# An FFN's weight splits: every second low half by ScalarE and an adding transfer, with the residual parked in HBM and two more weight buffers

## The chip, the cores and the metric

The kernel runs on one core of one Trainium2 chip. The metric is device microseconds of one execution. TensorE (PE) multiplies, VectorE (DVE) and ScalarE (ACT) do elementwise work, GpSimd (POOL) and SyncE (SP) issue transfers here, and 16 DMA engines move the data.

## The reference: what is computed

One layer of an encoder over 256 tokens of width 2048, all in float32. A mixing part (attention in a neighbourhood, and a recurrent block), then a SwiGLU feed-forward network (FFN) of width 5632, then an embedding of the layer's own. Each part ends in a normalisation and an addition to the residual `h`:

```
u  = rms_norm(h) @ w_in;  attn, rec = ...;  mixed = concat(norm(attn), norm(rec)) @ w_out
h  = h + rms_norm(mixed, g_mix_post)
fn = rms_norm(h, g_ffn_pre)
ff = (silu(fn @ w_ffn_gate) * (fn @ w_ffn_up)) @ w_ffn_down
h  = h + rms_norm(ff, g_ffn_post)
gate = sigmoid(rms_norm(h, g_ple_pre) @ w_ple_gate)
h  = h + rms_norm(gate * (p @ w_ple_proj), g_ple_post)
```

## The kernel before

**Three products for one.** PE multiplies float32 values in a reduced form, `fp32r`. To keep accuracy each operand is split into a high half (rounded to `fp32r`) and a low half (what is left), and each product is made of three: high by high, low by high, high by low (lines 601 to 603). The activations are split once. The weights are too large for that and are split as they stream through.

**A weight tile's way.** A tile is 512 KB: 128 partitions by two blocks of 512 columns. SP loads it into a raw buffer (`load_stream`, lines 489 and 506). ACT copies it into a high half `wh` (`hi_stream`, line 556). DVE subtracts to get the low half `wl` (`lo_stream`, line 569), which frees the raw buffer. PE uses a full tile in 12 matmuls of 128x512 (`products`) and then frees `wh` and `wl` (`free_w`). There are four raw buffers, three more in the FFN (`MORE_RAWS`, in the space of a gain vector and a spare tile), and four pairs of `wh` and `wl` (`W_BUFS`).

**The FFN.** Its 11 column groups of 512 are done in three parts of 4, 4 and 3. In each part every group has a gate chunk and an up chunk, whose product `mid` is transposed: DVE transposes blocks of 32x32 and 16 transfers of 32 KB move the blocks (`moved`, line 305; POOL issues 16 or 8 of them, SP the others). Then the down products of the part follow. Nine of the groups do a part of their products by a scheme with seven products in place of eight (`four_products`, `two_products`, `one_product`). Its tiles have 6 matmuls instead of 12, and some of its weight tiles are sums that DVE makes of loaded tiles (`sum_stream`, lines 526 to 537).

**What sets the order.** The order in which each engine gets its instructions is written by a planner (`Plan`): every stream is a generator that yields what it will use next (an engine and a cost, a buffer, or an event to wait for). The planner picks the step that can start first by its own clocks, with a bonus or a malus (`late`) for each stream. On the chip each engine then works through its own list in order and waits on semaphores.

**Around the FFN.** After the mix part `next_norm` adds the result to `h`, transposes it and makes the FFN's input halves. `h` (2 MB, a tile of the pool `rs`) is not touched again until the `next_norm` after the FFN.

Of the kernel before, what the change touches and what calls it, by code (L numbers as in the profile page):

```python
# [10 lines left out]
F32 = mybir.dt.float32  # L11
# [5 lines left out]
P = 128  # L17
S = 256
NT = S // P
# [29 lines left out]
W_BUFS = 4  # L49
R_BUFS = 4  # L50
MORE_RAWS = 3
SM_BUFS = 4
LATE = 0.8
EARLY = 3
# [1 line left out]
AHEAD = 5  # L56
ISSUE, LANDING = 160, 1.7
WARM = 9


class Event:
# [154 lines left out]
def layer(ctx: ExitStack, tc: tile.TileContext, a: dict, out: bass.AP):  # L216
# [5 lines left out]
    plan = Plan(wr=R_BUFS, w=W_BUFS, sm=SM_BUFS, acc=4, ev=1, mid=2, bt=2, m2=1, mt=1, sq=1, T=1, T4=1, **{f"wr{k}": 1 for k in range(MORE_RAWS)})  # L222

    def f32(t):
        return t.bitcast(F32)
# [13 lines left out]

    def raw_kind(i):  # L240
        return f"wr{more_raws[i]}" if i in more_raws else "wr"


    g_first = const.tile([P, KD], F32, name="g_first")
# [44 lines left out]
    def moved(e, here, take, tile_of, turn=True, pool=()):  # L289


        if turn:
            flat = e.rearrange("p t n -> p (t n)")
            yield dve(2 * N)
            nc.vector.transpose(out=flat, in_=flat)
        src = e.rearrange("p t (k j b) -> p t k j b", j=4, b=32)
        mT = None
        for j in range(4):
            for i in range(4):
                first = None if mT else take  # L300
                yield ("pool", 1.3, None, first, None) if i in pool else dma(150, take=first)
                if mT is None:
                    mT = tile_of()
                dst = mT.rearrange("p t k (i b) -> p t k i b", b=32)
                (nc.gpsimd if i in pool else nc.sync).dma_start(  # L305
                    dst[32 * j : 32 * j + 32, :, :, i, :],
                    src[32 * i : 32 * i + 32, :, :, j, :],
                )
        done(here)
        return mT.rearrange("p t k q -> p k t q")  # L310
# [230 lines left out]
    def hi_stream():  # L541
        for i in range(len(tiles)):
            at_hi[0] = i
            for j in pieces(i):
                n = j.stop - j.start
                yield ev_raw[i, j.stop]
                if i in big_w:
                    yield big_w[i][2]
                yield act(n * N, take=None if j.start or i in big_w else "w")
                if i in big_w:  # L550
                    his[i], los[i] = big_w[i][0](), big_w[i][1]()
                elif not j.start:
                    his[i] = wp.tile([P, 2, N], F32R, tag="wh", name="wh")
                    los[i] = wp.tile([P, 2, N], F32R, tag="wl", name="wl")
                src = raws[i][:, j, :]
                nc.scalar.copy(his[i][:, 0 : src.shape[1], :] if n == 2 else his[i][:, j, :], src)  # L556
                done(ev_hi[i, j.stop])

    def lo_stream():
        last_sum = max(f[0] for f in fours.values())  # L560
        for i in range(len(tiles)):
            at_lo[0] = i
            for j in pieces(i):
                n = j.stop - j.start
                yield ev_hi[i, j.stop]
                src = raws[i][:, j, :]
                m = slice(j.start, j.start + src.shape[1])
                yield dve(src.shape[1] * N, give=gives.get(i) or raw_kind(i) if j.stop == 2 else None)
                nc.vector.tensor_tensor(  # L569
                    out=los[i][:, m, :], in0=src, in1=f32(his[i][:, m, :]), op=ALU.subtract  # L570
                )
# [828 lines left out]
    def next_norm(sub, nxt, rstd, ev_rstd, g_next):  # L1400
# [49 lines left out]
        nc.vector.tensor_reduce(out=tot, in_=ssh, op=ALU.add, axis=AX.X)  # L1450
        yield from rstd_of(tot, D, rstd, rt)
        done(ev_rstd)

    TURNED = 3

    def turn_h(c, hi, lo, nxt, gname):
# [8 lines left out]
        for b in range(4):  # L1465
            kk = 4 * c + b
            yield from gained_split(
                *(x[:, kk, :].rearrange("p (t q) -> p t q", t=NT) for x in (hi, lo)), mT[:, b],
                col(gname, kk), give="mt" if b == 3 else None,
            )  # L1470
            done(nxt.ev[kk])

    def next_gain(g, ready):
        yield from load_gain(g[1])
# [476 lines left out]
```

## Time and profile before

| what | us |
|---|---|
| median of 3 runs (1174.24 to 1177.76) | 1175.87 |
| span of the profiled execution | 1171.8 |
| PE busy | 1158.1 |
| DVE busy | 819.2 |
| ACT busy | 672.7 |
| POOL busy | 89.1 |

The runs' times lie about 4 us above the span of the profiled execution, which is counted from its first to its last instruction; the page gives no other time of that execution. Over the whole span the DMA engines move 250.90 MB, 214 GB/s on average.

A row of the table of stretches gives, for a stretch in microseconds from the start of the span, the busy time and number of instructions of each engine, the granted clock of PE, the mean share in which the 16 DMA engines were busy (it is a sum of packet times, and can pass 1), and the GB/s moved. A group row gives line, engine, operation, operands, number, then busy time and mean ns, then the idle time ahead and what ended it. A row of the waits gives engine and line, what they waited for, the sum in us, the number of times and the longest. A row of the chain gives start, length, and what it was.

### The profile page before, as it was taken

How to read it: one execution, taken by the hardware profiler on the slowest of the kernel's cores; microseconds unless marked ns; L12 is line 12 of the kernel's file. 1: busy time of each engine (PE TensorE's matmuls, PEld its weight loads, DVE VectorE, ACT ScalarE, POOL GpSimd, SP SyncE). 2: the span in 40 equal slices, each digit the busy share in tenths (PEclk: the TensorE clock that was granted, in tenths of full speed). 3: DMA queues.
4: the chain of work that ended last, by engine and by line, in shares of the span. 5: the costliest groups of instructions: out<-in, count | busy, mean ns of one | idle time of the engine just before them, and what ended most of it. 6: DMA issues, size and time to landing. Idle time of an engine off the chain costs nothing.

```text
span 1171.8 us, 14922 instructions
## 1 busy us (share of the span) xinstructions
PE 1158.1 (99%) x5276; PEld 960.0 (82%) x5276; DVE 819.2 (70%) x997; ACT 672.7 (57%) x891; POOL 89.1 (8%) x163
## 2 busy tenths in 40 slices
PE   9999999999999999999999999999999999999997
PEld 7888888888888878888888887888888888887786
DVE  6678787898468767855567777765677785568565
ACT  6777777875556645554445554544344554456564
POOL 0000000000000203111000203210000302100000
PEclk9999999999999999999999999999999999999999
DMA  8868566446765778687566777778556877754762
GB/s 304 307 176 233 175 191 199 162 162 208 242 241 163 248 240 253 216 243 203 176 233 209 236 250 204 245 213 223 196 200 225 240 223 228 215 190 158 235 222 76
DMA packets 108714, 250.90 MB, mean 214 GB/s; under 512 B 38880, under 2 KB 45792, under 8 KB 108000
## 3 DMA queue, kind: packets, MB, share of 16 engines
q1 hardware_dynamic: 103344, 244.62, 66.3%
q0 software_dynamic: 4864, 4.99, 1.7%
q8 instruction: 41, 0.67, 0.2%
q14 instruction: 33, 0.27, 0.1%
q10 hardware_dynamic: 432, 0.35, 0.1%
HBM read 239.42 MB, written 2.10 MB: 206 GB/s over the span
## 4 chain that ended last, share of the span: by engine, by line
PE 91%; DMA 3%; DVE 3%; ACT 2%; issue 1%; SPq 1%; ACTq 0%; DVEq 0%
PE acc L603 27%; PE acc L602 27%; PE acc L601 27%; PE acc L614 2%; PE acc L612 2%; PE acc L613 2%; DVE wl L569 1%; DMA wr<-in_w_ffn_up 1%; PE tr L286 1%; ACT wh L556 1%; DMA sq<-ev 1%; DMA more<-in_w_ffn_up 1%; DMA xs<-in_xT 0%; PE pg L317 0%; PE pg L318 0%
## 5 line engine op out<-in xcount | busy, mean ns | idle before, releaser
L569 DVE TENSOR_TENSOR wl<-wr,wh 128x1024 fp32r<-128x1024 f32 (+1 forms) x320 | 383.2, 1210 | 172.1 <-ACT wh L556 168.6
L556 ACT CAST wh<-wr 128x1024 fp32r<-128x1024 f32 (+1 forms) x320 | 332.4, 1044 | 256.9 <-PE acc L602 203.9
L603 PE MATMUL acc<-wl,hT_mix_hi 128*128 128x512 f32 x560 | 218.3, 390 | 2.9 <-DVE wl L569 2.9
L602 PE MATMUL acc<-wh,hT_mix_lo 128*128 128x512 f32 x560 | 218.1, 389 | 0.3 <-DVE hT_mix_lo L275 0.3
L601 PE MATMUL acc<-wh,hT_mix_hi 128*128 128x512 f32 x560 | 218.2, 390 | 0.0
L305 POOL DMA_DIRECT2D mT<-mid x152 | 87.9, 585 | 916.8 <-DMA wr<-in_w_ffn_gate 529.0
L603 PEld LDWEIGHTS acc<-wl,hT_mix_hi 128*128 128x128 f32 x560 | 105.1, 188 | 26.3 <-DVE wl L569 4.5
L603 PE MATMUL acc<-wl,hT_hi 128*128 128x512 f32 x320 | 124.8, 391 | 0.1
L601 PE MATMUL acc<-wh,hT_hi 128*128 128x512 f32 x316 | 124.4, 394 | 0.0
L602 PEld LDWEIGHTS acc<-wh,hT_mix_lo 128*128 128x128 f32 x560 | 105.1, 188 | 22.7 <-DVE hT_mix_lo L275 1.0
L602 PE MATMUL acc<-wh,hT_lo 128*128 128x512 f32 x316 | 123.2, 390 | 0.0
L601 PEld LDWEIGHTS acc<-wh,hT_mix_hi 128*128 128x128 f32 x560 | 105.1, 188 | 21.5
L556 ACT CAST wh<-more 128x1024 fp32r<-128x1024 f32 x60 | 63.3, 1054 | 69.5 <-PE acc L602 64.6
L569 DVE TENSOR_TENSOR wl<-more,wh 128x1024 fp32r<-128x1024 f32 x60 | 72.8, 1221 | 38.9 <-ACT wh L556 36.6
L603 PEld LDWEIGHTS acc<-wl,hT_hi 128*128 128x128 f32 x320 | 60.1, 188 | 13.5 <-DVE wl L569 0.8
L602 PEld LDWEIGHTS acc<-wh,hT_lo 128*128 128x128 f32 x316 | 59.4, 188 | 11.7
L601 PEld LDWEIGHTS acc<-wh,hT_hi 128*128 128x128 f32 x316 | 59.4, 188 | 11.4
L556 ACT CAST wh<-ple 128x1024 fp32r<-128x1024 f32 x27 | 28.5, 1055 | 39.5 <-PE acc L602 34.0
L569 DVE TENSOR_TENSOR wl<-third,wh 128x1024 fp32r<-128x1024 f32 x31 | 37.9, 1221 | 17.8 <-ACT wh L556 17.1
L556 ACT CAST wh<-third 128x1024 fp32r<-128x1024 f32 x31 | 32.7, 1053 | 30.0 <-PE acc L602 23.9
L601 PE MATMUL acc<-wh,mid0h 128*128 128x512 f32 x128 | 49.8, 389 | 0.0
L602 PE MATMUL acc<-wh,mid0l 128*128 128x512 f32 x128 | 49.8, 389 | 0.0
(338 smaller groups left out, 1963.2 us busy)
## 6 DMA issues: line engine op xcount, KB each, us to landing
wr<-in_w_in SPq DMA_DIRECT2D x77, 512.0 KB, 4.6
wr<-in_w_ffn_gate SPq DMA_DIRECT2D x58, 512.0 KB, 4.6
wr<-in_w_ffn_up SPq DMA_DIRECT2D x58, 512.0 KB, 4.6
wr<-in_w_ffn_down SPq DMA_DIRECT2D x57, 512.0 KB, 4.2
wr<-in_w_out SPq DMA_DIRECT2D x32, 512.0 KB, 4.3
wr<-in_w_ple_gate SPq DMA_DIRECT2D x32, 512.0 KB, 4.6
more<-in_w_ffn_down SPq DMA_DIRECT2D x21, 512.0 KB, 4.2
more<-in_w_ffn_gate SPq DMA_DIRECT2D x20, 512.0 KB, 4.7
```

The costliest lines, as they stand in the source:

```text
L286: nc.tensor.transpose(tr[:, b, t * P : (t + 1) * P], e[:, t, sl], ident)
L305: (nc.gpsimd if i in pool else nc.sync).dma_start(dst[32 * j : 32 * j + 32, :, :, i, :], src[32 * i : 32 * i + 32, :, :, j, :],)
L556: nc.scalar.copy(his[i][:, 0 : src.shape[1], :] if n == 2 else his[i][:, j, :], src)
L569: nc.vector.tensor_tensor(out=los[i][:, m, :], in0=src, in1=f32(his[i][:, m, :]), op=ALU.subtract)
L601: nc.tensor.matmul(accs[t], hi[:, sl], his[i][:, j, :], start=st, stop=False, **group)
L602: nc.tensor.matmul(accs[t], lo[:, sl], his[i][:, j, :], start=False, stop=False, **group)
L603: nc.tensor.matmul(accs[t], hi[:, sl], los[i][:, j, :], start=False, stop=sp, **group)
L612: nc.tensor.matmul(dst, x[0], wh, start=start, stop=False, skip_group_check=seeded)
L613: nc.tensor.matmul(dst, x[1], wh, start=False, stop=False, skip_group_check=seeded)
L614: nc.tensor.matmul(dst, x[0], wl, start=False, stop=stop, skip_group_check=seeded)
```

## The change

For every second full weight tile of the FFN (from the fifth tile after the start of the seven-product scheme, `by_dma`), DVE no longer makes the low half. ACT, after its copy to the high half, writes the negated high half into `los[i]` (an activation with scale -1, which gives the raw buffer back), and POOL then issues a DMA that reads the same weight tile from HBM again and adds it into `los[i]`. That gives weight minus high half. There are 101 such tiles.

Two more pairs of weight buffers are used from the same tile on until 24 tiles ahead of the end of the FFN's list (`more_w`, `LAST_W`). They lie in the space of `h`, four halves of 4 KB per partition: `h` is written to HBM after the mix part (`spill_h`) and read back into a new tile when PE has used the last tile of the added buffers (`reload_h`). The `next_norm` after the FFN waits for that.

The planner's cost of a move on POOL goes from 1.3 to 0.65 us, and an accumulation is planned with 1.0 us on POOL and a landing 2.5 us later than the planner's usual latency. PE's instructions and their order stay.

```diff
+MORE_W = 2
+ACCUMULATED = 2
+LAST_W = 24
...
+ACC_ISSUE, ACC_LANDING = 1.0, 2.5
+MOVE_ISSUE = 0.65
...
+    def w_kind(i):
+        return f"w{more_w[i]}" if i in more_w else "w"
+
+    def w_tiles(i):
+        if i not in more_w:
+            return [wp.tile([P, 2, N], F32R, tag=t, name=t) for t in ("wh", "wl")]
+        if "w" not in t2:
+            t2["w"] = t2["pool"].tile([P, 4 * MORE_W, N], F32R, tag="h", name="w")
+        k = 4 * more_w[i]
+        return t2["w"][:, k : k + 2, :], t2["w"][:, k + 2 : k + 4, :]
...
-                yield ("pool", 1.3, None, first, None) if i in pool else dma(150, take=first)
+                yield ("pool", MOVE_ISSUE, None, first, None) if i in pool else dma(150, take=first)
...
+                if i in more_w:
+                    yield ev_spilled
+                yield act(n * N, take=None if j.start or i in big_w else w_kind(i))
...
                 nc.scalar.copy(his[i][:, 0 : src.shape[1], :] if n == 2 else his[i][:, j, :], src)
+                if i in by_dma:
+                    yield act(n * N, give=raw_kind(i))
+                    nc.scalar.activation(los[i], src, AF.Copy, scale=-1.0)
+                    plan.add(accumulated(i), plan.now, -2 * SOON)
                 done(ev_hi[i, j.stop])
+
+    def accumulated(i):
+        yield ("pool", ACC_ISSUE, None, None, None)
+        nc.gpsimd.dma_start(los[i], by_dma[i], accum_op=ALU.add)
+        plan.now += ACC_LANDING
+        done(ev_lo[i, 2])
...
                 yield ev_hi[i, j.stop]
+                if i in by_dma:
+                    continue
...
     def free_w(i):
         if i not in keep:
-            plan.free["w"].append(plan.clk["pe"])
+            plan.free[w_kind(i)].append(plan.clk["pe"])
+        if more_w and i == max(more_w):
+            plan.add(reload_h(), plan.clk["pe"], -SOON)
...
-        yield ev_h
+        yield ev_h if sub is mix else ev_back
...
+        if sub is mix:
+            for e in nxt.ev:
+                yield e
+            plan.add(spill_h(), plan.now)
...
+    def spill_h():
+        yield dma(2048)
+        nc.sync.dma_start(spill, t2["h"])
+        done(ev_spilled)
+
+    def reload_h():
+        yield dma(2048)
+        t2["h"] = t2["pool"].tile([P, NT, D], F32, tag="h", name="h")
+        nc.sync.dma_start(t2["h"], spill)
+        done(ev_back)
...
+    for i in range(min(fours) + 4, i_ple - LAST_W):
+        n += 1
+        if n % (W_BUFS + MORE_W) < MORE_W:
+            more_w[i] = n % (W_BUFS + MORE_W)
+    n = 0
+    for i in range(min(fours) + 4, i_ple):
+        tl = tiles[i]
+        if isinstance(tl, tuple) and i not in fours and i - 1 not in fours:
+            n += 1
+            if n % ACCUMULATED == 0:
+                w, k, n0 = tl
+                by_dma[i] = a[w][n0 // N, k // 2]
```

More of the change, by code (lines that the diff above doesn't have):

```diff
@@ L221, in layer @@
     ps = ctx.enter_context(tc.tile_pool(name="ps", bufs=4, space=bass.MemoryType.PSUM))
-    plan = Plan(wr=R_BUFS, w=W_BUFS, sm=SM_BUFS, acc=4, ev=1, mid=2, bt=2, m2=1, mt=1, sq=1, T=1, T4=1, **{f"wr{k}": 1 for k in range(MORE_RAWS)})
+    plan = Plan(wr=R_BUFS, w=W_BUFS, sm=SM_BUFS, acc=4, ev=1, mid=2, bt=2, m2=1, mt=1, sq=1, T=1, T4=1, **{f"{w}{k}": 1 for w, n in (("wr", MORE_RAWS), ("w", MORE_W)) for k in range(n)})
     def f32(t):
@@ L241, in raw_kind @@
         return f"wr{more_raws[i]}" if i in more_raws else "wr"
+    more_w = {}
+    by_dma = {}
+    def w_kind(i):
[7 more added lines that the diff above has]
+        return t2["w"][:, k : k + 2, :], t2["w"][:, k + 2 : k + 4, :]
     g_first = const.tile([P, KD], F32, name="g_first")
@@ L548, in hi_stream @@
                     yield big_w[i][2]
-                yield act(n * N, take=None if j.start or i in big_w else "w")
+                if i in more_w:
+                    yield ev_spilled
+                yield act(n * N, take=None if j.start or i in big_w else w_kind(i))
                 if i in big_w:
@@ L552, in hi_stream @@
                 elif not j.start:
-                    his[i] = wp.tile([P, 2, N], F32R, tag="wh", name="wh")
-                    los[i] = wp.tile([P, 2, N], F32R, tag="wl", name="wl")
+                    his[i], los[i] = w_tiles(i)
                 src = raws[i][:, j, :]
                 nc.scalar.copy(his[i][:, 0 : src.shape[1], :] if n == 2 else his[i][:, j, :], src)
+                if i in by_dma:
+                    yield act(n * N, give=raw_kind(i))
+                    nc.scalar.activation(los[i], src, AF.Copy, scale=-1.0)
+                    plan.add(accumulated(i), plan.now, -2 * SOON)
                 done(ev_hi[i, j.stop])
+    def accumulated(i):
[3 more added lines that the diff above has]
+        done(ev_lo[i, 2])
     def lo_stream():
@@ L1471, in turn_h @@
             done(nxt.ev[kk])
+    spill = ctx.enter_context(
+        tc.tile_pool(name="spill", bufs=1, space=bass.MemoryType.DRAM)
+    ).tile([P, NT, D], F32, name="h_spill")
+    ev_spilled, ev_back = Event(), Event()
+    def spill_h():
[7 more added lines that the diff above has]
+        done(ev_back)
     def next_gain(g, ready):
@@ L1837, in layer @@
                 more_raws[i] = n % (R_BUFS + MORE_RAWS)
+    n = 0
[3 more added lines that the diff above has]
+            more_w[i] = n % (W_BUFS + MORE_W)
+    n = 0
+    for i in range(min(fours) + 4, i_ple):
[5 more added lines that the diff above has]
+                by_dma[i] = a[w][n0 // N, k // 2]
     for i, (last, _, _, _) in fours.items():
```

## The prediction

> **What bounds the kernel now.** I read the page's totals first, then busy time by stretch, then who waits for whom.
>
> ```profile
> span 1171.8 us, 14922 instructions
> ...
> PE 1158.1 (99%) x5276; PEld 960.0 (82%) x5276; DVE 819.2 (70%) x997; ACT 672.7 (57%) x891; POOL 89.1 (8%) x163
> ...
> PE 91%; DMA 3%; DVE 3%; ACT 2%; issue 1%; SPq 1%; ACTq 0%; DVEq 0%
> ```
>
> PE is busy for all but 13.7 us, and 91% of the chain that ended last is PE. A busy PE could still be a slow one, so the next view gives matmuls by stretch: the FFN from 384 to 1066 us, cut at its up/gate and down phases (528 to 620, 785 to 877 and 998 to 1066 are the three down phases), and three stretches of the input projection with heavy loading.
>
> ```profile
> core 0: us, PE busy (x) PEld busy (x) DVE busy (x) ACT busy (x) POOL busy (x), PEclk, DMA share, GB/s
> 28.00:38.00 10.00, 10.00 (x46) 8.27 (x45) 5.40 (x7) 8.28 (x13) 0.00 (x0) 1.00 1.02 415
> 26.00:46.00 20.00, 20.00 (x90) 16.57 (x89) 12.07 (x14) 15.48 (x23) 0.00 (x0) 1.00 0.93 350
> 0.00:50.00 50.00, 48.77 (x215) 40.27 (x216) 29.41 (x40) 36.29 (x53) 1.20 (x11) 1.00 0.89 317
> ...
> 384.00:1064.00 680.00, 677.10 (x2984) 559.69 (x2983) 465.44 (x475) 340.10 (x370) 87.92 (x152) 1.00 0.72 221
> 384.00:528.00 144.00, 142.13 (x625) 116.90 (x624) 101.64 (x108) 74.84 (x82) 27.88 (x48) 1.00 0.76 238
> 528.00:620.00 92.00, 92.00 (x407) 76.20 (x406) 54.18 (x54) 42.90 (x47) 4.61 (x8) 1.00 0.67 206
> 620.00:785.00 165.00, 163.97 (x723) 135.49 (x723) 121.75 (x124) 87.53 (x95) 27.72 (x48) 1.00 0.76 229
> 785.00:877.00 92.00, 92.00 (x407) 76.20 (x407) 57.04 (x59) 39.62 (x40) 4.61 (x8) 1.00 0.67 206
> 877.00:998.00 121.00, 121.00 (x536) 100.22 (x535) 89.27 (x91) 63.32 (x67) 18.50 (x32) 1.00 0.73 226
> 998.00:1066.00 68.00, 68.00 (x302) 56.32 (x301) 42.86 (x46) 33.82 (x46) 4.61 (x8) 1.00 0.64 197
> ```
>
> In a down phase 407 matmuls take 92.00 us, 0.226 us each, at a granted clock of 1.00 and without a gap; the other FFN rows give the same pace. So the FFN has 680.00 - 677.10 = 2.9 us of idle PE, and that is the most that any help to ACT, DVE or the loads can win there. DVE, which the change relieves, is busy 465 of 680 us and ACT 340: neither is the bound. Who waits, in the FFN:
>
> ```profile
> PE acc L603 <- DVE wl L569: 2.9, 3, 1.4
> ```
> ```profile
> SPq L489 <- DVE wl L569: 455.9, 215, 7.4
> ```
> ```profile
> 716.82 1.06 ACT wh L556
> ...
> 717.90 1.24 DVE wl L569
> ...
> 719.89 0.70 DVE wr L537
> ...
> 720.61 6.03 DMA wr<-in_w_ffn_up
> ...
> 728.10 1.23 DVE wl L569
> ...
> 729.37 0.50 PE acc L603
> ```
>
> The 2.9 us are three stalls. The chain ahead of the one at 729 shows their make: a raw buffer comes free late (719.89 plus 0.70), its load then takes 6.03 us, and the low half reaches PE late. SP's row says that loads always wait for DVE to free a raw buffer.
>
> **The change, part by part.** PE's instructions stay the same and in the same order: 0 us.
>
> *The low halves.* Of the FFN's full tiles, every second one loses its L569 subtraction: 101 tiles (56 of up, 44 of down, 1 of the embedding). Each gets a second ACT copy with scale -1 and an accumulating DMA from POOL that reads the tile's 512 KB from HBM again.
>
> ```profile
> L569 DVE TENSOR_TENSOR wl<-wr,wh 128x1024 fp32r<-128x1024 f32 x314 | 379.2, 1220 | 171.3 <-ACT wh L556 167.8 <-PE acc L603 1.3
> L556 ACT CAST wh<-wr 128x1024 fp32r<-128x1024 f32 x314 | 328.7, 1052 | 255.7 <-PE acc L602 203.9 <-DMA wr<-in_w_ple_gate 8.9 <-PE acc L613 7.5
> L305 POOL DMA_DIRECT2D mT<-mid x152 | 87.9, 585 | 916.8 <-DMA wr<-in_w_ffn_gate 529.0 <-DVE mid L295 235.5 <-DMA more<-in_w_ffn_gate 129.4
> ```
>
> DVE: 101 x 1.22 = 123 us less, of 465. ACT: 101 x 1.05 = 106 us more, 446 of 680. POOL: 101 issues at the 0.585 us of a move, 59 us more, 147 of 680. All three stay under the 680 us of PE work, which covers them; uncovered, ACT's 106 us would be the price, and that needs ACT to be full. The raw buffer of such a tile is freed by ACT's copy instead of by DVE.
>
> *What the DMA engines get.* The trace has no accumulating DMA. From below it costs what a load costs: 512 KB of transfer, 101 x 0.524 = 53 MB. From above I count two loads, because the add must read the weights and what lies in the tile: 106 MB of engine time. I take the upper one, since one transfer and one read of the same size is nearest to two load rows. In MB per us this adds to the rows above, by the phase in which the tiles fall (15, 15, 25, 16, 18, 12 tiles), with 1.049 MB a tile:
>
> - 384 to 528: 238 + 109 = 347, and 362 with the parked residual (2.1 MB)
> - 528 to 620: 206 + 171 = 377
> - 620 to 785: 229 + 159 = 388
> - 785 to 877: 206 + 182 = 388
> - 877 to 998: 226 + 156 = 382
> - 998 to 1066: 197 + 185 + 31 (the residual's 2.1 MB back) = 413
>
> What can the engines do? The row from 26 to 46 moves 350 GB/s at a share of 0.93, which makes 350/0.93 = 376 at a full share; the 50 us row makes 317/0.89 = 356; the best 10 us reach 415. I take 376, the middle one. (The FFN's own 221/0.72 = 307 is no limit, since the rows above exceed it; its shares hold latencies too.) Where demand exceeds 376 over a whole phase, no buffer helps, and PE gets its tiles at the rate of the transfers. The phases grow by 92 x 0.3% = 0.2, 165 x 3.2% = 5.3, 92 x 3.2% = 2.9, 121 x 1.6% = 1.9 and 68 x 9.8% = 6.7 us: 17.0 us. By 356 the six terms are 2.4, 5.4, 14.8, 8.3, 8.8, 10.9 = 51 us; by 415, or with one load's cost instead of two (at most 229 + 79 = 308, or 320 with the residual), 0.
>
> [...]
>
> *The longer way to a low half.* PE now waits for a transfer instead of a DVE subtraction.
>
> ```profile
> wr<-in_w_ffn_down SPq DMA_DIRECT2D x57, 512.0 KB, 4.2
> mT<-mid POOLq DMA_DIRECT2D x152, 32.0 KB, 6.2
> ```
> ```profile
> L489 SPq DMA_DIRECT2D wr<-in_w_ffn_down x57: 327/328/689, 509.7 to 1044.4; - x57
> ...
> DMA to landing us min/median/max: 3.3/4.5/9.3
> ```
> ```profile
> POOL mT L305 <- DMA mT<-mid: 19.7, 20, 2.1
> ```
>
> From PE's release of a weight buffer: high half 1.05, negated copy 1.05, some 0.3 of hand-overs, then from issue to landing 4.5 us (a load's median) at least, 9.3 (its longest) at most; I take the median plus a second reading of 0.524 MB at 376 GB/s, 1.4 us: 5.9. That makes 8.3 us (6.9 to 11.7). What PE gives: with six buffers the five tiles between take 12 matmuls of 0.226 each (6 where two tiles share a seven-product step), 9.9 us at seven places and 11.3 to 14.0 elsewhere, counted to the third matmul, which first reads the low half. In the last 24 tiles there are four buffers again: 3 x 2.71 + 0.45 = 8.6 us. So 8.3 fits everywhere, with 0.3 us to spare in the tail: 0 us. At 11.7 the tail loses 3.1 us in each turn of its four buffers, 6 x 3.1 = 19, and the seven places 7 x 1.8 = 13: 32 us. POOL's queue is in order: an accumulation behind 11 moves (6.4 us, and waits of up to 2.1 us for earlier moves to land) would miss 11.3 us; the order written puts it ahead of them, after five at most (2.9 us).
>
> *Residual and buffers.* The write after the mix stage and the read near the end are counted in the first and last phase. SP's weight loads queue behind each; 2.1 MB is 5.6 us at 376. Raw tiles run some eight tiles (21.7 us) ahead, which covers it; uncovered, 5.6 us each. The read is needed only after the last down tile, some 60 us later. High halves that use the new buffers wait for the write on ACT; the planner puts them 30 tiles into the FFN, after it: 0.
>
> *The stalls.* Earlier free raw buffers help where the transfers have room, which is the first phase: 144.00 - 142.13 = 1.9 us won. The stall at 729 lies in a phase that I count as full and stays.
>
> **Sum.** 1171.8 + 17.0 - 1.9 = 1186.9 us of span. The median of the runs, 1175.87, is 4.1 us above the profiled span; with that, 1191.
>
> **The rivals.**
>
> *Hidden (no change).* The accumulation costs a load, or the engines hold 400 and more. For it: 415 GB/s over 10 us, and PE without a gap at shares of 0.76. Against it: 350 is the best over 20 us. Everything lands in time, and 1.9 to 2.9 us of stalls go: 1173 to 1174 (up to 1179 with a stray stall). [...]
>
> *Late, not full (slower).* The transfers have room, but an accumulation lands later than 8.6 us allows in the tail and 9.9 at the seven places: 1175.9 + 10 to 32 = 1186 to 1208. For it: 6.2 us for 32 KB on POOL's queue, 0.3 us to spare. Against it: the load median. It decides from 6.2 us of issue to landing.
>
> *Faster by over 0.3% (3.5 us).* All 2.9 us of FFN stalls go, and with DVE less loaded also some 0.7 us of those after 1066 us: 1172. Against it: it needs all of them.
>
> **How the numbers follow.** About 0.3% is what a measurement of this kernel can tell. Full engines 0.42 (own range 1180 to 1227, and 1191 within it), late 0.20, hidden 0.32, faster 0.06. Slower is 0.42 + 0.20 = 0.62. The range goes from the hidden case with all stalls gone, 1172, to 356 GB/s with part of the late case, 1175.9 + 51 + 5 = 1232.
>
> **What would show it.** A DMA share of 0.9 or more in the down phases; idle PE of 5 to 10% there, put down to the accumulating DMA or to loads of wr; landing of in_w_ffn_down on POOL's queue near 6 us; no stall at 432 and 472. Right would be more PE idle in the last phase than in the first. Wrong: shares under 0.85 with PE gapless (hidden), or stalls in the last 24 tiles only at shares under 0.85 (late). An accumulation that takes three transfers' time would put the time beyond 1232.

## The result and the profile after

The changed kernel takes 1249.03 us (median of 4 runs, 1247.5 to 1252.56) against 1176.3 us before on the same chip: a ratio of 1.0626, 95% interval 1.0601 to 1.0651. It is 73 us slower. The forecast was 1191 us, and its range ended at 1232.

First the page's totals of the changed kernel: span, busy time by engine, the two queues that carry data (packets, MB, share of 16 engines over the span; q1 is SP's, q0 is POOL's), and the chain that ended last.

```profile
span 1246.2 us, 15098 instructions
...
PE 1182.5 (95%) x5276; PEld 969.7 (78%) x5276; DVE 698.9 (56%) x896; ACT 762.9 (61%) x992; POOL 180.9 (15%) x264
...
q1 hardware_dynamic: 103632, 248.81, 59.8%
q0 software_dynamic: 19408, 57.95, 24.0%
...
PE 60%; DMA 22%; issue 12%; DVE 2%; ACT 2%; POOL 2%; SPq 0%; POOLq 0%; DVEq 0%; ACTq 0%
```

DVE lost 120 us of work, where the prediction counted 123. ACT gained 90 (106) and POOL 92 (59), since an accumulation's issue takes 0.87 us and not the 0.585 of a move. DMA now holds 22% of the chain, which was 91% PE. The same two queue rows of the kernel before:

```profile
q1 hardware_dynamic: 103344, 244.62, 66.3%
q0 software_dynamic: 4864, 4.99, 1.7%
```

q0 gained 52.96 MB, 101 transfers of 512 KB. Its packets' time rose from 0.017 x 16 x 1171.8 = 319 to 0.240 x 16 x 1246.2 = 4785 us summed over the engines, so an accumulation costs 44.2 us of engine time. A load costs 0.663 x 16 x 1171.8 / 244.62 x 0.524 = 26.6 us, by the mean of all that its queue moves. By single packets of 4 KB, the median is 0.328 us for an adding one and 0.159 us for a loading one.

Next, busy time by stretch in the FFN, with the new limits of its phases. The down products start at 543.8, 821.8 and 1052.4 us, so 544 to 645, 822 to 923 and 1052 to 1143 are the down phases:

```profile
core 0: us, PE busy (x) PEld busy (x) DVE busy (x) ACT busy (x) POOL busy (x), PEclk, DMA share, GB/s
384.00:544.00 160.00, 148.87 (x622) 120.39 (x621) 83.92 (x92) 90.16 (x99) 42.79 (x64) 0.96 0.97 282
544.00:645.00 101.00, 95.76 (x412) 78.50 (x411) 36.07 (x38) 57.08 (x63) 17.94 (x23) 0.97 0.97 266
645.00:822.00 177.00, 168.52 (x720) 136.42 (x719) 91.74 (x99) 108.79 (x119) 50.56 (x73) 0.98 1.02 287
822.00:923.00 101.00, 95.48 (x411) 78.23 (x411) 39.14 (x44) 54.59 (x57) 18.91 (x24) 0.97 0.94 267
923.00:1052.00 129.00, 121.89 (x532) 98.99 (x531) 64.94 (x71) 75.61 (x82) 34.06 (x49) 1.00 1.01 285
1052.00:1143.00 91.00, 76.41 (x324) 60.20 (x323) 32.85 (x43) 47.44 (x63) 15.40 (x20) 0.98 0.92 250
384.00:1143.00 759.00, 706.93 (x3012) 572.73 (x3011) 348.66 (x383) 433.68 (x479) 179.67 (x253) 0.98 0.98 276
```

The share of the DMA engines went from 0.72 to 0.98. PE idles in every phase, 52 us in all, most in the last one (14.6 of 91 us), and the granted clock is below 1.00 in five of the six. Who waits, and how long transfers take from issue to landing (median, last column):

```profile
PE acc L635 <- DMA wl<-in_w_ffn_down: 23.1, 10, 5.2
PE acc L635 <- DMA w<-in_w_ffn_up: 17.5, 10, 3.5
PE acc L635 <- DMA wl<-in_w_ffn_up: 5.8, 7, 2.3
PE acc L635 <- DVE wl L601: 3.7, 4, 2.8
```
```profile
wr<-in_w_ffn_gate SPq DMA_DIRECT2D x58, 512.0 KB, 7.2
wr<-in_w_ffn_up SPq DMA_DIRECT2D x58, 512.0 KB, 6.7
wr<-in_w_ffn_down SPq DMA_DIRECT2D x57, 512.0 KB, 7.7
...
wl<-in_w_ffn_up POOLq DMA_DIRECT2D x32, 512.0 KB, 9.2
wl<-in_w_ffn_down POOLq DMA_DIRECT2D x32, 512.0 KB, 8.3
```

An accumulation lands 8.4 us after its issue (median; 7.3 to 13.9), and the loads of `wr` beside it went from between 4.2 and 4.6 us to between 6.7 and 7.7 us. The first packet of an accumulation starts 3.7 us after the issue (median), and its packets spread over another 4.

Last, what the lost time is made of. I took all of the FFN's matmuls, from the first product of its input to the first product behind it, and compared each gap between two starts with the 0.227 us of a matmul at full pace. Before, gaps of 0.23 us too much or more (stalls) make 3.8 us; after, 59.6 us in 38 stalls, 53.7 of them at tiles whose low half an accumulation makes. Another 14.0 us are 70 matmuls 0.427 us apart. The chain shows the first and the last of eleven such matmuls behind the longest stall (start, length, what):

```profile
571.30 8.27 DMA wl<-in_w_ffn_down
...
579.62 0.80 PE acc L635
580.41 0.43 PE acc L633
...
585.10 0.23 PE acc L635
```

So the FFN's 74 us (718.9 to 793.0) are 56 us more of stalls, nearly all on accumulated low halves, 14 us of half pace behind them, and some 4 us of smaller gaps. Of the 53.7 us, 16 lie at the tiles of the tail, which have four buffers, 15 at six tiles whose transfer POOL issued 1.8 to 4.1 us late, 10 at two tiles for which ACT's queue was held, and 12 at thirteen others. Measured by their own matmuls (the first from the FFN's first product on, the last to the first product behind the FFN), the six phases grew by 17, 8, 13, 8, 9 and 19 us.

The half pace goes with a granted clock of 0.50. Two stretches, the first with the stall that ends at 451.6 us, show it (columns as above):

```profile
448.42:451.83 3.41, 1.30 (x6) 0.81 (x5) 3.41 (x4) 3.41 (x5) 0.00 (x0) 1.00 1.05 300
451.83:455.24 3.41, 3.41 (x9) 2.66 (x9) 0.41 (x2) 0.25 (x1) 0.87 (x1) 0.50 1.03 317
```

### The profile page after: what moved, and what is told of

Same layout as the page of the kernel before. It is cut to its first block, busy times and chain, and to the rows that moved or that the text cites. A ratio compares the mean times of both kernels' runs of the same rounds, so it can differ in the third digit from the quotient of the medians.

```text
span 1246.2 us, 15098 instructions
## 1 busy us (share of the span) xinstructions
PE 1182.5 (95%) x5276; PEld 969.7 (78%) x5276; DVE 698.9 (56%) x896; ACT 762.9 (61%) x992; POOL 180.9 (15%) x264
## 4 chain that ended last, share of the span: by engine, by line
PE 60%; DMA 22%; issue 12%; DVE 2%; ACT 2%; POOL 2%; SPq 0%; POOLq 0%; DVEq 0%; ACTq 0%
PE acc L635 18%; PE acc L634 17%; PE acc L633 17%; DMA wl<-in_w_ffn_down 6%; DMA wl<-in_w_ffn_up 6%; DMA w<-in_w_ffn_up 4%; DMA mT<-mid 2%; DVE wl L601 1%; PE acc L645 1%; PE acc L644 1%; PE acc L646 1%; POOL mT L324 1%; DMA third<-in_w_ffn_up 1%; PE tr L305 1%; DMA w<-in_w_ffn_down 1%
## 5 line engine op out<-in xcount | busy, mean ns | idle before, releaser
L576 ACT CAST wh<-wr 128x1024 fp32r<-128x1024 f32 (+1 forms) x279 | 288.2, 1041 | 202.9 <-PE acc L634 127.9
L601 DVE TENSOR_TENSOR wl<-wr,wh 128x1024 fp32r<-128x1024 f32 (+1 forms) x234 | 279.6, 1207 | 182.9 <-ACT wh L576 174.7
L635 PE MATMUL acc<-wl,hT_mix_hi 128*128 128x512 f32 x376 | 148.7, 395 | 9.5 <-DMA wl<-in_w_ffn_up 5.8
L634 PE MATMUL acc<-wh,hT_mix_lo 128*128 128x512 f32 x376 | 147.4, 392 | 0.3 <-DVE hT_mix_lo L294 0.3
L633 PE MATMUL acc<-wh,hT_mix_hi 128*128 128x512 f32 x376 | 147.4, 392 | 0.0
L635 PE MATMUL acc<-w,hT_mix_hi 128*128 128x512 f32 x184 | 75.9, 413 | 17.6 <-DMA w<-in_w_ffn_up 17.5
L633 PE MATMUL acc<-w,hT_mix_hi 128*128 128x512 f32 x184 | 74.5, 405 | 0.0
L634 PE MATMUL acc<-w,hT_mix_lo 128*128 128x512 f32 x184 | 74.2, 403 | 0.0
L576 ACT CAST w<-wr 128x1024 fp32r<-128x1024 f32 x41 | 43.0, 1049 | 38.9 <-PE acc L634 28.2
L635 PEld LDWEIGHTS acc<-w,hT_mix_hi 128*128 128x128 f32 x184 | 36.3, 197 | 29.7 <-DMA w<-in_w_ffn_up 22.2
L601 DVE TENSOR_TENSOR wl<-more,wh 128x1024 fp32r<-128x1024 f32 x27 | 32.9, 1222 | 43.6 <-ACT wh L576 43.4
```

Of the source, the lines that this page charges most:

```text
L601: nc.vector.tensor_tensor(out=los[i][:, m, :], in0=src, in1=f32(his[i][:, m, :]), op=ALU.subtract)
L633: nc.tensor.matmul(accs[t], hi[:, sl], his[i][:, j, :], start=st, stop=False, **group)
L634: nc.tensor.matmul(accs[t], lo[:, sl], his[i][:, j, :], start=False, stop=False, **group)
L635: nc.tensor.matmul(accs[t], hi[:, sl], los[i][:, j, :], start=False, stop=sp, **group)
```

## The experiments

Two theories at first. **A, full engines:** the adding doubles the engines' time, loads come late as a whole, and PE gets tiles at the transfers' rate. **B, lateness:** each accumulation lands after PE wants it, at its own place, and the way it takes through the in-order queues of POOL and ACT decides. All ratios are to the kernel before on the same chip, with 95% intervals.

### The adding taken away, the residual alone, half the transfers, no tail

```diff
-        nc.gpsimd.dma_start(los[i], by_dma[i], accum_op=ALU.add)
+        nc.gpsimd.dma_start(los[i], by_dma[i])
```

> The changed kernel with the adding transfer turned into a plain one of the same 512 KB on the same queue (the low half then holds the weights themselves, so the result is not the layer's; the work of all engines is otherwise the same). Theory A, the second read fills the DMA engines: a packet of 4 KB falls from 0.33 to 0.16 us, the share of the DMA engines in the FFN falls from 0.98 to under 0.88, and the time to 1173 to 1185 us. Theory B, not the engines but the way through POOL is long (issue, first packet some 3.5 us later, landing): an accumulation lands after 7.4 us instead of 8.7, the tail with four buffers keeps at least 8 of its 17 us of stalls, and the time is 1195 to 1225 us.

1189.53 us, 1.0114 (1.0086 to 1.0143). Of 73 us, 60 go with the adding alone; the queue, the order of instructions and the bytes written are the same. Its q0 row and landings:

```profile
q0 software_dynamic: 19408, 57.95, 15.0%
...
wr<-in_w_ffn_up SPq DMA_DIRECT2D x58, 512.0 KB, 5.1
...
wl<-in_w_ffn_up POOLq DMA_DIRECT2D x32, 512.0 KB, 7.0
```

A copying transfer takes (0.150 x 16 x 1187.8 - 319) / 101 = 25.1 us of engine time against 44.2. Stalls fall to 18.6 us. The time lies above what A gave and below what B gave, and of neither theory did the sign come as it was put: the FFN's share is 0.91, not under 0.88, and a landing is 7.0 us, below the 7.4 of B. The adding sets both the engines' time and the landing, so this run can't part the two.

```diff
-            if n % ACCUMULATED == 0:
+            if n % ACCUMULATED == ACCUMULATED:
```

> Only the parked residual, the two more weight pairs and the planner's new cost of a move; no accumulation, DVE makes all low halves. Both theories: the accumulations carry the loss, so 1173 to 1177 us, with one or two of the three stalls of before gone. If parking or the added buffers carry a part of the loss, over 1180 us.

1175.37 us, 0.9988 (0.9973 to 1.0002): the parked residual and the two added pairs cost nothing and bring nothing.

```diff
-ACCUMULATED = 2
+ACCUMULATED = 4
```

> Every fourth full tile accumulates instead of every second (50 instead of 101). Theory A: transfers with the second read counted fall to some 310 MB per us and stay under what the engines reached in the changed kernel (346), so nearly all stalls go but those of the tail: 1178 to 1195 us. Theory B: half of the late tiles stay late, so half of the loss: 1205 to 1218 us.

1216.93 us, 1.0349 (1.0313 to 1.0384). With 50 accumulations 40 of the 73 us are still there, as B had it; a capacity that is merely exceeded at 101 would have set most of it free. A landing still takes 8.2 us.

```diff
-    for i in range(min(fours) + 4, i_ple):
+    for i in range(min(fours) + 4, i_ple - LAST_W):
         tl = tiles[i]
```

> Every second full tile accumulates, but none of the last 24, which have four buffers. Both theories: the 17 us of stalls in the last down phase go and a part of the half-speed matmuls there, 1228 to 1236 us. If the four buffers are the main cause of the loss, under 1210; if the tail's stalls only make up for waits that come later anyway, over 1242.

1228.93 us, 1.0436 (1.0389 to 1.0484), as expected: the 12 accumulations of the tail, where there are four buffers, cost 20 us.

### One place of lateness at a time

In the changed kernel ACT makes the high half, then the negated copy. Here the two are exchanged, so that the transfer is issued about 1 us earlier:

```diff
-                nc.scalar.copy(his[i][...], src)
                 if i in by_dma:
-                    yield act(n * N, give=raw_kind(i))
                     nc.scalar.activation(los[i], src, AF.Copy, scale=-1.0)
                     plan.add(accumulated(i), plan.now, -2 * SOON)
+                    yield act(n * N, give=raw_kind(i))
+                nc.scalar.copy(his[i][...], src)
```

> The changed kernel with the negated copy ahead of the copy to the high half, so that each adding transfer is issued some 1.0 us earlier; bytes, engines and order otherwise the same. Theory A, the DMA engines are full over whole phases: nothing is won, 1244 to 1253 us. Theory B, each transfer is late against the fixed lead that the weight buffers give (8.6 to 14 us from release to use, 10.1 to 13.4 needed where PE stalls): each of the 29 stalls at an accumulated tile shrinks by up to 1.0 us, 24 us in all, and some half-speed matmuls behind them go: 1212 to 1230 us.

1237.63 us, 1.0518 (1.0464 to 1.0573): 11 us less, where B gave 19 to 37 and A nearly nothing. The FFN's stalls fall from 59.6 to 53.0 us.

```diff
-LAST_W = 24
+LAST_W = 8
```

> The two added weight pairs stay in use until 8 tiles ahead of the end instead of 24, so the last down phase has six buffers too, and the residual is read back later. Theory B: the lead there grows from 8.6 to 14 us and most of the 17 us of stalls go: 1228 to 1238 us. Theory A: the last phase has as many bytes as before, its stalls stay: 1244 to 1255 us.

1243.9 us, 1.058 (1.0548 to 1.0612): only 5 us, next to A's range. The stalls of the first tail tiles went, and others came: one of 2.0 us where ACT's queue was held for 10.2 us, and two of 3.0 and 3.6 us near the end.

Where ACT's queue is held, a view of its instructions in the changed kernel shows best (start, length, instruction, and in brackets the idle time before it):

```profile
555.70 1.05 ACT L579 ACTIVATE wl<-wr 128x1024 fp32r<-128x1024 f32 x1
567.00 1.14 ACT L286 CAST mid0h<-mT 128x512 fp32r<-128x512 f32 x2 [10.25 <-DMA wr<-in_w_ffn_down]
568.05 2.00 ACT L576 CAST wh<-wr 128x1024 fp32r<-128x1024 f32 x2
569.95 1.05 ACT L579 ACTIVATE wl<-wr 128x1024 fp32r<-128x1024 f32 x1
```

ACT stands 10.25 us at a copy of `mT`, which the moves fill (the load named is the one that landed last by the profile; the copy reads `mT` alone). Three weight copies queue behind it, and the negated copy that ends at 571 leads to the 5.40 us stall at 579.6. In the next kernel such copies get a due time 10 us later:

```diff
-            plan.add(carried(mid, kk0, mT), plan.now + (0.5 if soon else 3.0), -SOON if soon else SOON)
+            plan.add(carried(mid, kk0, mT), plan.now + (10.0 if soon else 3.0), -SOON if soon else SOON)
```

> The planner takes the copies of the last transposed mid block of a part for ready 10 us after the moves instead of 0.5, so they stand later in ACT's list. Theory B with ACT's queue blocked (8 to 9 us from release to high half at the stalls of 5.4 and 4.9 us early in the first two down phases): these two stalls and the half-speed matmuls behind them go, 1230 to 1240 us. If the block is only a sign of full engines, the stalls move elsewhere: 1244 to 1253 us.

1233.75 us, 1.0483 (1.0457 to 1.0509): 15 us, as B had it. The stalls of 5.40 and 4.88 us are gone.

```diff
-            mT = yield from moved(e, there, "mt", mT_tile, pool=(0, 2) if soon else range(4))
+            mT = yield from moved(e, there, "mt", mT_tile, pool=())
```

> All moves of mid blocks are issued by SP, none by POOL, so no accumulation waits behind a move or for its landing. Theory B: the six accumulations that POOL issued 1.8 to 4.1 us late come in time, 12 to 16 us of stalls go: 1232 to 1240 us, less if the weight loads behind the moves on SP come late; then 1245 to 1260 us.

1265.7 us, 1.0769 (1.0744 to 1.0795): 17 us worse, and above both ranges. With the moves in SP's queue, among its loads, ACT stands 81 us at its copies of `mT`, against 44 in the changed kernel, so the high halves behind them are held longer. To relieve POOL's queue at the cost of SP's did not pay.

### Places mended together

> The changed kernel with two of its places of lateness mended at once: the negated copy stands before the high half's copy, and the two copies that wait for the moves are given to ScalarE's queue 10 us later. All 101 adding transfers stay. Alone they gave 11.4 and 15.2 us. If lateness is the whole cause (B) the gains add, 1220 to 1226 us. If the engines are full (A) the time freed at one place is lost at the next, 1230 to 1240 us.

1226.25 us, 1.0433 (1.0373 to 1.0493), just above B's range: 23 us by the medians, of the 26.7 that the two gave alone.

> As the run with the negated copy first and the copies behind the moves later, and no accumulation in the last 24 tiles (89 left), which alone gave 20 us. B: the three gains add, 1200 to 1208 us, and the low halves that are still late are those whose issue POOL's queue holds back. A: the 89 transfers keep some 38 us of the loss, 1212 to 1225 us.

1211.15 us, 1.0277 (1.0248 to 1.0305): 38 us of the 46.8 that the three gave alone; between B's 1200 to 1208 and A's 1212 to 1225, and nearer to A's. What is left shows in two stretches of it, the first with the whole first down phase (537 to 630), the second in the up/gate phase behind it:

```profile
528.00:640.00 112.00, 112.00 (x496) 92.78 (x495) 43.99 (x46) 70.92 (x78) 21.38 (x27) 1.00 1.03 291
640.00:810.00 170.00, 160.67 (x680) 129.41 (x679) 87.23 (x95) 101.45 (x112) 48.80 (x71) 0.97 1.01 284
```

At a share of 1.03 PE has no gap for 112 us. The packets of 18.6 accumulations lie in them, so with each of these counted as two loads, as in the prediction, it is 291 + 87 = 378 GB/s there. So a share of 1 is not by itself a stall. In the up/gate phase, at 1.01, PE loses 9 us, and there POOL also issues the moves. POOL's queue ahead of the stall at 522.6 us, and ACT's at the same time:

```profile
507.00 1.15 POOL L324 DMA_DIRECT2D mT<-mid  x2 [0.56 <-DMA mT<-mid]
512.18 1.16 POOL L324 DMA_DIRECT2D mT<-mid  x2 [4.03 <-DMA wl<-in_w_ffn_up]
513.64 0.94 POOL L585 DMA_DIRECT2D w<-in_w_ffn_up  x1 [0.30 <-issue]
```
```profile
507.60 1.06 ACT L577 ACTIVATE w<-wr 128x1024 fp32r<-128x1024 f32 x1 [1.89 <-PE acc L635]
508.56 1.98 ACT L580 CAST w<-wr 128x1024 fp32r<-128x1024 f32 x2
```

The negated copy is done at 508.7, and its transfer is issued 5 us later, behind a move that by the profile waits 4.03 us for an earlier adding transfer to land. At six of the seven longest stalls of this kernel the issue is 2.1 to 5.2 us late in this way, where it is otherwise 0.3.

Half the transfers in the same kernel (`ACCUMULATED = 4`):

> The kernel with both places mended and no accumulation in the tail (1211 us with 89 adding transfers), with every fourth tile accumulated in place of every second, some 44 transfers. The engines' time falls by some 44 x 128 x 0.328 us over 16 engines, 115 us. If the 33 us that are left of the loss are engines that are full (A), nearly all of it goes: 1176 to 1184 us. If each accumulation pays for its own late sum (B), half of it goes: 1192 to 1198 us.

1192.27 us, 1.0118 (1.0069 to 1.0166). Half of the rest went, as B had it (by the medians; one of the four runs took 1183 us). Then the seven tiles with the longest stalls left out (`i - 114 not in (48, 65, 137, 156, 173, 245, 262)` in the condition of `by_dma`), and as a control seven others (37, 56, 126, 145, 164, 234, 253):

> The kernel with both places mended and no accumulation in the tail (1211 us, 89 adding transfers), less seven accumulations: those that PE waited for longest there (2.40, 3.76, 2.13, 1.59, 4.29, 3.18 and 3.73 us, 21 of its 29 us of waits), six of them because POOL's queue issued the transfer 2.1 to 5.2 us after the negated copy, behind the moves. VectorE makes these seven low halves again. 82 transfers stay. If the cost is sums that are late at their own place (B), 21 us of waits and some 6 us of matmuls at half pace behind them go: 1183 to 1190 us. If the engines' time decides (A), seven of 89 are worth 3 us and the waits turn up elsewhere: 1204 to 1211 us.

> The control to the run before: seven other accumulations of the same phases are taken away, for which PE did not wait. The engines' time is the same in both. B: 1207 to 1213 us. A: the same time as with the other seven gone.

1204.1 us, 1.0244 (1.0215 to 1.0274), and 1215.94 us, 1.0348 (1.0312 to 1.0383). With the same engine time the choice of tiles makes 11.8 us, so the places decide too, and A in its pure form falls. What at those places is less sure: the control came out 5 us slower than with all 89, and the planner wrote POOL's list in another order in it. In the control 14 transfers are issued over 1.5 us after their negated copy, with all 89 it is nine, and without the seven it is three. So the 11.8 us are of the tiles and of that order together. And the seven waited-for tiles gave back 7 us by the medians (4 by the ratios) where B said 21 to 28. PE's two longest sums of waits without the seven:

```profile
PE acc L635 <- DMA wl<-in_w_ffn_up: 8.0, 6, 2.4
PE acc L635 <- DVE wl L601: 7.2, 6, 2.8
```

The waits for accumulations in up tiles were 22.1 us (16.7 and 5.4) before the seven were left out. The stalls at the seven are gone, and shorter ones stand at other tiles, some of them now behind DVE: 24.2 us of stalls in all, against 29.3.

### Transfers that nobody waits for

Here A and B differ by 40 us. DVE makes every low half as before, in four pairs; the 89 transfers and their negated copies go into spare targets in the parked residual's space, and no matmul reads them:

```diff
-                    nc.scalar.activation(los[i], src, AF.Copy, scale=-1.0)
-                    plan.add(accumulated(i), plan.now, -2 * SOON)
+                    k = 2 * (list(by_dma).index(i) % 4)
+                    nc.scalar.activation(t2["w"][:, k : k + 2, :], src, AF.Copy, scale=-1.0)
+                    plan.add(accumulated(i, t2["w"][:, k : k + 2, :]), plan.now, -2 * SOON)
...
-        nc.gpsimd.dma_start(los[i], by_dma[i], accum_op=ALU.add)
+        nc.gpsimd.dma_start(to, by_dma[i], accum_op=ALU.add)
```

> The residual is parked as in the change, but VectorE computes every low half again, in four weight pairs and in the rotation of before. The 89 adding transfers of the kernel without its tail's accumulations are still issued, with their negated copies on ScalarE and at the same places of the stream, but into four spare targets in the parked residual's space which no matmul reads; their sums are thrown away and the result is still the layer's. Against the kernel that uses those 89 sums (1228.9 us): if the DMA engines' time is what costs (theory A, full engines), the loads come late all the same and it takes 1215 to 1230 us, with PE waiting for wr or wh. If the cost is that a low half arrives after PE wants it (theory B, lateness), no matmul waits for an adding transfer and it takes 1174 to 1187 us, at a DMA share still near 0.9 in the FFN's phases.

1231.29 us, 1.0463 (1.0434 to 1.0493). B falls as the whole cause: unused transfers cost as much as 89 used ones did (1228.93 us). Then the same without the adding (`accum_op` dropped), the same with the copies behind the moves 10 us later, and the negated copies alone, with no transfer:

> As the run with 89 adding transfers that nobody uses, with one word changed: they copy instead of adding, so that queue, order, bytes written and ScalarE's negated copies stay and only the second read and the adding go (an adding packet took 0.328 us in the changed kernel, a copying one on the same queue 0.174). If the DMA engines' time is what the unused transfers cost (theory A), most of the 53 us goes: 1177 to 1190 us. If it is the place that they and their copies take in the queues of POOL and ScalarE (theory B'), little changes: 1215 to 1231 us. The result is still the layer's.

> As the run with 89 unused adding transfers, and the two copies that wait for the moves are given to ScalarE's queue 10 us later (the waits of 6.6, 9.8 and 3.0 us at wh behind them made 19 of its 47 us of waits). If these are lateness of ScalarE alone, 1206 to 1214 us. If the engines' time is the floor under it (A), the freed time is lost again at the loads, above all at the sums on VectorE that wait for one: 1218 to 1229 us.

> As the run with 89 unused copying transfers, without the transfers: ScalarE still makes the 89 negated copies at their places, POOL issues nothing for them. If the unused transfers cost through the DMA engines and POOL's queue, all of the 53 (adding) and 33 us (copying) are theirs and this takes 1174 to 1180 us. If ScalarE's copies, which delay the high halves behind them by 1 us each, are what costs, 1195 to 1208 us. The result is still the layer's.

1208.63 us, 1.0258 (1.0210 to 1.0307); 1227.58 us, 1.0435 (1.0407 to 1.0463); 1175.46 us, 1.0017 (0.9995 to 1.0038). ACT's 89 copies are free. All of the 53 and 33 us belong to the transfers and their places in POOL's queue. The adding is worth some 20 us of the 53 here, less than A said; the copying transfers already cost 33. How a transfer that nobody reads delays PE is seen in three kinds of waits, of the kernels with no transfer (which has none of the third kind), with copying ones and with adding ones, in this order:

```profile
DVE ple L545 <- DMA wr<-in_w_ffn_up: 10.7, 8, 3.6
ACT mid1h L286 <- DMA third<-in_w_ffn_down: 5.6, 1, 5.6
```
```profile
DVE ple L545 <- DMA wr<-in_w_ffn_up: 26.3, 9, 7.6
ACT mid1h L286 <- DMA third<-in_w_ffn_down: 12.3, 1, 12.3
POOL mT L324 <- DMA w<-in_w_ffn_up: 26.6, 9, 4.5
```
```profile
DVE ple L545 <- DMA wr<-in_w_ffn_up: 38.0, 10, 7.0
ACT mid1h L286 <- DMA third<-in_w_ffn_down: 17.1, 1, 17.1
POOL mT L324 <- DMA w<-in_w_ffn_up: 34.7, 10, 5.0
```

The FFN's share of the DMA engines is 0.73, 0.89 and 0.95 in them (384 to 1075, 1105 and 1125 us), and a load of the up weights lands in 4.3, 5.4 and 6.4 us. Each longer landing meets an in-order queue: DVE stands at a sum of loaded tiles with other tiles' low halves behind it, ACT at the copy behind the moves with high halves behind it. The third row is POOL's own queue: its moves wait for earlier transfers of the same queue to land, and a move of POOL lands in 5.6, 7.3 and 8.4 us in the three kernels, one of SP in 4.6, 5.2 and 5.1. So the full engines are not the only way in; no run has the same transfers on another queue, and how the 33 us divide between the engines' load and POOL's queue is open. When ACT's copies behind the moves are given 10 us more, 4 us are won and the waits turn up elsewhere, as A had it.

### What a stall of PE costs beyond itself

The kernel before, with nothing of the change; at eleven tiles ACT repeats the high half's copy 6 to 16 times:

```diff
+                for _ in range(REPEATS.get(i, 0)):
+                    nc.scalar.copy(his[i][...], src)
```

> The kernel before, with nothing of the change. At eleven tiles of the FFN ScalarE repeats the copy of the high half 6 to 16 times, so that PE waits there once for some 1 to 8 us and is then served at once. It measures what a wait of PE costs beyond itself: in the changed kernel waits of 2.2 to 5.4 us were followed by ten to sixteen matmuls at 0.427 us in place of 0.227. If a wait of some length brings this about, the same is seen here behind the waits beyond that length, up to 3 us each; if it was the adding transfers' doing, no matmul behind these waits is slow.

All nine stalls of 2.65 to 14.27 us are followed by 3 to 12 matmuls 0.427 us apart; none of the four of 1.56 to 1.72 us is. One of them (start, length, instruction):

```profile
745.72 0.80 PE L604 MATMUL acc<-wh,hT_mix_hi 128*128 128x512 f32 x1 [9.39 <-ACT acc L657]
746.32 0.63 PE L605 MATMUL acc<-wh,hT_mix_lo 128*128 128x512 f32 x1
746.74 0.63 PE L606 MATMUL acc<-wl,hT_mix_hi 128*128 128x512 f32 x1
...
749.30 0.40 PE L606 MATMUL acc<-wl,hT_mix_hi 128*128 128x512 f32 x1
749.54 0.40 PE L604 MATMUL acc<-wh,hT_mix_hi 128*128 128x512 f32 x1
```

So the half pace follows a wait of PE without any adding transfer. In the changed kernel it is 6 to 12 matmuls behind eight of the stalls, and not the ten to sixteen of the expectation. The one execution took 1264.4 us.

The clock records of all 20 traces part the cases more sharply than the length of a stall does. In the FFN of the changed kernel all changes of the granted clock lie whole multiples of 3.413 us apart (the nearest 3.413, the farthest 245.76, which is 72 of them). A stretch is here one such step. In the FFNs, 97 stretches at full clock were followed by one at 0.5, and PE stalled for 1.89 us or more in each of them; of the other stretches at full clock with that much idle time there were only four, of 1.96 to 2.06 us. A stall of 3.47 us that fell half into one stretch and half into the next, in the kernel without seven others, left the clock at 1.00.

## Why the prediction was wrong

The direction was right, and the time was 17 us beyond the range. Step by step:

- **What bounds the kernel, and PE's instructions.** Right: without the transfers PE stays the bound (1175.37 us).
- **DVE, ACT and POOL under cover.** DVE's busy time came as counted, ACT's 16 us under and POOL's 33 us over it, and none of it is full. That ACT's copies are covered held (89 of the negated copies alone: 1175.46 us). But the cover was argued from busy time, and what failed is order: ACT stood 10.25 us at one copy behind the moves. Later due times for such copies gave 15 us.
- **An accumulation costs two loads.** Nearly right: 44.2 against 26.6 us of engine time, 1.7 loads; a packet 2.06 (0.328 us against 0.159). It was the right end to take. No run shows the second reading itself, which was the author's estimate; the runs show these times alone.
- **A ceiling of 376 GB/s (written as MB per us), hence 17 us.** The value was reached: with places mended, PE ran 112 us without a gap at 291 GB/s, or 378 with each accumulation counted as two loads, so no run shows that a phase grows for this reason. Counted like that, the FFN of the changed kernel has 276 + 70 = 346 at a share of 0.98, that is 353 at a full one. With 353 the six terms would be 57 us and the sum 1231, but it is the rate of an FFN that stalled, and not a ceiling. The prediction's growth by phase (0, 0.2, 5.3, 2.9, 1.9, 6.7) is not the measured one (17, 8, 13, 8, 9, 19): the first phase, priced at a gain of 1.9, lost 17. The row of ten us at 415 GB/s was reached in no whole phase.
- **The longer way to a low half: 5.9 us, hence 0 us.** This is the step that failed. It measured 8.4 us (7.3 to 13.9), and its upper bound, the longest load of a kernel at a share of 0.72, lay barely above the median. PE's stalls on accumulated tiles are 53.7 us, where the sum has 0. The term before it had the engines full, and this one took the landing of a load beside engines that were not. At a share of 0.98 in place of 0.72 the loads take longer too (4.6 to 6.7 us in the up tiles). The size of the landing is a part of the failure alone: with 8.4 the prediction's own count gives 10.8 us against 8.6 and 9.9, some 13 us in the tail, where 16 were measured, and 6 us at the seven places, while the stalls outside the tail make 38. Of these, 25 stand where the order of work made the transfer late: 15 behind POOL's moves and 10 behind ACT's held queue.
- **Two rivals that exclude each other.** "Full" and "late, not full" were priced apart, with lateness only at shares below 0.85. Lateness came at shares of 0.92 to 1.02. The 6.2 us of landing from which lateness was to decide were passed by all of them (the shortest took 7.3). That the tail suffers was right (20 us for its 12 accumulations).
- **POOL's order, at most 2.9 us.** In the changed kernel six of the tiles that PE stalled at were issued 1.8 to 4.1 us late, which makes 15 us. The sum had 0.
- **Residual and buffers, 0.** Right: 0.9988 (0.9973 to 1.0002).
- **Stalls of the first phase, 1.9 us won.** Wrong: the stall at 472 went, but the one at 432 grew from 1.57 to 2.96 us, four new ones came at accumulated tiles, and the phase idles 11.1 us.
- **Not priced:** 14.0 us of matmuls at half pace behind the stalls.
- **What was to show it.** Shares above 0.9, idle PE of 5 to 10% in the down phases (5.2, 5.5 and, in the last, 16%) and most idle in the last phase: all seen, though they came from late transfers, and not from the rate for which they were named. Landing near 6 us was not seen, and one of the two stalls stayed.

What of the two theories stands: the transfers are the root (no transfers, no loss; without the adding 60 of 73 us go). They act by making single transfers late against queues that work in order, and not by a plain shortage of rate (PE without a gap at a share of 1.03). How much of this lateness is the load on the DMA engines and how much the place in POOL's queue, no run parts. Mending places, and leaving out the tail's 12 accumulations, gives back 38 us, and then the waits move on. That the last 29 us (82 transfers, 1204.1 us) could be mended as well, or are the rate's, was not settled. Nor is it shown why 89 unused copying transfers cost 33 us and 101 used ones 13; the kernel with unused ones has four weight pairs and all low halves on DVE, so less slack, but slack alone was not varied. No version here beats the kernel before.

## What to carry to other kernels

A transfer that replaces an engine's work should be priced by its landing among the transfers that will then run, not by the landings of the kernel before (here 8.4 us at a share of 0.98, where 5.9 was priced from loads at 0.72); set that landing against the lead of every consumer, starting where buffers are fewest (8.6 us in the tail). Look for the in-order queues where one late transfer holds unrelated work (here a copy behind moves on ACT, 10.25 us, an issue behind moves on POOL, 1.8 to 4.1 us late, a sum on DVE, up to 7.0 us beside the unused adding transfers), since busy time does not show them. A test with the same transfers and no reader tells whether a loss is theirs or the reader's.

## What the runs showed of the hardware

- In the FFN of the changed kernel the granted clock of PE went to 0.50 eight times, five times for 3.41 us and three times for 6.83; 128x512 matmuls then started 0.427 us apart in place of 0.227. This followed eight stalls of 2.17 to 5.40 us and not four others of 2.09 to 2.54, and cost, there and in the kernel with made stalls, 0.6 to 2.4 us each time (3 to 12 matmuls, 0.2 us each). In the FFNs of all 20 traces it followed all of 85 stretches of 3.41 us with more than 2.06 us of idle PE in them, 12 of 16 with 1.89 to 2.06, and none with less.
- An adding packet of 4 KB took 0.328 us, 2.06 times a loading one (0.159) and 1.9 times a copying one on the same queue (0.174, in the run without the adding). The whole transfer's engine time was 44.2 us against 25.1 for a copy on the same queue, 1.8 times.
- Dropping the adding alone took the landing on POOL's queue from 8.4 to 7.0 us, still above the 5.1 us of SP's loads of up weights in the same kernel; the first packet of a copy came 2.6 us after its issue, and that of an adding one 3.7.
